# Two more products of seven in each MLP down projection of a two-layer decoder trunk, hidden parts kept for a second use, and weight pieces placed behind a norm

## The chip, the core and the metric

The kernel runs on one core of a Trainium2 chip. The engines named below are PE (TensorE, matrix products), DVE (VectorE), ACT (ScalarE), POOL (GpSimd) and SP (SyncE, which here issues the weight loads). The metric is the device time of one execution in microseconds (us), as a median over several runs.

## The reference

Two decoder layers over 256 tokens of width 2048, in float32. Layer 0 has stick-breaking attention, layer 1 differential attention over a key/value projection of its input. Each layer adds a scaled residual, normalizes, and then runs an MLP with 8192 hidden columns and normalizes again:

```python
def squared_relu_mlp(x, w_up, w_down):
    h = jax.nn.relu(x @ w_up)
    return (h * h) @ w_down
...
for layer in range(DEPTH):
    if layer < N_A_LAYERS:
        h = stick_breaking_attention(x, sb_w_qkv[layer], sb_w_o[layer])
    else:
        if layer == N_A_LAYERS:
            k_shared, v_shared = shared_kv(x, kv_w)
        ...
        h = differential_attention(x, k_shared, v_shared, ...)
    x = layer_norm(DEEPNORM_ALPHA * x + h, ln_g[layer, 0], ln_b[layer, 0])
    x = layer_norm(DEEPNORM_ALPHA * x + squared_relu_mlp(x, mlp_w_up[layer], mlp_w_down[layer]),
                   ln_g[layer, 1], ln_b[layer, 1])
```

The change touches the MLP's down projection, `(256 x 8192) @ (8192 x 2048)`, in both layers, and the seam from layer 0's last norm to layer 1's key/value projection.

## The kernel before

**Products of split numbers.** PE multiplies in a float32 form of reduced precision (fp32r). Every operand is split in two: ACT writes the high part (`split`, L60), and DVE the low part, source minus high part (L63). A product is three matmuls: high·high, high·low, low·high (`three`). For a weight the parts are called `wh` and `wl`; a load lands in `st` (four buffers, `ST_BUFS`), and `wh`, `wl` come from a ring of seven (`W_BUFS`).

**The down projection** (in `mlp`). The 8192 rows are worked in 32 pairs of 128-row groups, and the 2048 columns in two halves of 1024 (`nh` = 0, 1). `main` and `side` are accumulators in PSUM. An ordinary (classic) pair loads two pieces of 512 KB, splits them to `wh`/`wl`, splits the hidden values to `hp` (`hidden`, three buffers), and issues 24 matmuls of 128x512. For some pairs, listed in `SEVEN`, `seven` does the same 2x2 block product with seven products of three matmuls instead of eight: 21 matmuls. It needs sums and differences of the weight blocks and of the hidden values (DVE, L331 to L340), and splits of these: `hi` and `lo` of `raw` (the loaded 1 MB block, in whose last quarter the differences of hidden values are put), and `wh`, `wl` of the two halves of `sums`. `raw`, `sums`, `hi` and `lo` come from the four buffers of the tag `xT`, which hold the layer's transposed input at other times. After the last seven of a half, `share_out` adds the accumulators of `side` to the outputs with nine DVE operations. Before the change the sevens are each third pair: nine in the first half of the columns, eight in the second, 17 of 64 in a layer.

The last five pairs of the second half (`lag` = 10 groups) are worked by token block, so that the first block's output is ready early: `rest` (L377, L378) adds the residual and gathers statistics, and `layernorm` follows. Its aggregate is L139, `ve` L141, `rstd` on POOL L143, and the two halves of the normalization are L147 and L148 in four pieces of 512 columns; then PE transposes each piece (L97), and ACT and DVE split it to `xT`.

**The seam.** Layer 1 begins with the values' projection, `by_token` over `kv_w` (L639): eight chunks of weights, in four runs of two, and in each run first the products of token block t = 0 and then of t = 1. Its first matmuls run while DVE still normalizes block t = 1.

**Order.** Each engine runs its instructions in the order in which they stand in its queue. That order is set when the program is built, by the framework's scheduler from its own costs and due times; the kernel's source gives the instructions and what they depend on. Waits between engines are semaphores, buffers come from pools, and an instruction that needs a buffer waits until its last reader is done.

Of the kernel before, what the change touches and what calls it, by code (L numbers as in the profile page):

```python
# [2 lines left out]

# [8 lines left out]
ALU = mybir.AluOpType  # L12
# [17 lines left out]
RUN = 2  # L30
ST_BUFS = 4
W_BUFS = 7
SEVEN = ((3, 6, 9, 12, 15, 18, 21, 24, 27), (3, 6, 9, 12, 15, 18, 21, 24))


@with_exitstack
def trunk(ctx: ExitStack, tc: tile.TileContext, x, ln_g, ln_b, sb_w_qkv, sb_w_o, kv_w, diff_w_q,
# [96 lines left out]
    def new_stats():  # L134
        return [small.tile([P, 4, 6], F32, tag="stats", bufs=2, name=nm("stats")) for _ in range(NT)]

    def layernorm(t, stats, gb, last=False):
        mv = small.tile([P, 2], F32, tag="mv", bufs=2, name=nm("mv"))
        nc.vector.bn_aggr(mv, stats.rearrange("p a b -> p (a b)"))  # L139
        ve = small.tile([P, 1], F32, tag="ve", bufs=2, name=nm("ve"))  # L140
        nc.vector.tensor_scalar(ve, mv[:, 1:2], EPS, None, op0=ALU.add)  # L141
        rstd = small.tile([P, 1], F32, tag="rstd", bufs=2, name=nm("rstd"))
        nc.gpsimd.tensor_tensor(rstd, ve, neghalf[:, :1], op=ALU.pow)  # L143
        for j in range(4):
            sl = slice(j * 512, (j + 1) * 512)
            y = xs[:, t, sl]
            nc.vector.scalar_tensor_tensor(y, y, mv[:, 0:1], gb[j][0], op0=ALU.subtract, op1=ALU.mult)  # L147
            nc.vector.scalar_tensor_tensor(y, y, rstd, gb[j][1], op0=ALU.mult, op1=ALU.add)  # L148
# [5 lines left out]
    def mm(o, l, r, start, stop):  # L154
        nc.tensor.matmul(o, l, r, start=start, stop=stop)  # L155

    def by_token(w, n0, staggered=False, between=None):

        accs = [acc() for _ in range(NT)]
        run = RUN if staggered else 1  # L160
        for c0 in range(0, KT // 2, run):
            chunks = [
                wchunk(w[2 * c * P:(2 * c + 2) * P, n0:n0 + 512].rearrange("(a p) n -> p a n", p=P))
                for c in range(c0, c0 + run)
            ]
            for t in range(NT):
                ts = slice(t * P, (t + 1) * P)
                if between and c0 == 0 and t == 1:
                    between()
                for c, (wh, wl) in zip(range(c0, c0 + run), chunks):  # L170
                    for kk in range(2):
                        k = 2 * c + kk
                        mm(accs[t], xT[k // 4][:, k % 4, 0, ts], wh[:, kk, :], k == 0, False)
                        mm(accs[t], xT[k // 4][:, k % 4, 0, ts], wl[:, kk, :], False, False)
                        mm(accs[t], xT[k // 4][:, k % 4, 1, ts], wh[:, kk, :], False, k == KT - 1)
            tick()
        return accs
# [90 lines left out]
    def mlp(layer, last):  # L268
        up, down = mlp_w_up[layer], mlp_w_down[layer]
        with tc.tile_pool(name=f"mlp{layer}", bufs=1) as pool:  # L270
# [15 lines left out]
            def gb_of(j):  # L286
                piece = pool.tile([P, 2, 512], F32, tag="hT", bufs=FT // 4, name=nm("gb"))
                return piece[:, 0, :], piece[:, 1, :]
# [89 lines left out]
                nc.vector.bn_stats(stats[t][:, n, :], y)  # L378

            fast = SEVEN  # L380
            gb = []
            side = [acc() for _ in range(4)]
            main = [[acc("at"), acc("at")], [acc("at"), acc()]]
            for nh in range(2):
                n0 = nh * CH
                if nh == 1:
# [2 lines left out]
                        for n in range(2):  # L389
                            rest(t, n, old[t][n])  # L390
                    side = [acc("at"), acc("at"), acc("at"), acc()]
                for j in range(FT // 2 - (lag // 2 if nh else 0)):
                    k = 2 * j
                    if nh == 1 and FT // 4 < j <= FT // 4 + 4:
                        i = j - FT // 4 - 1
                        gb.append(gb_of(i))
                        for piece, src in zip(gb[i], (ln_g, ln_b)):
                            nc.vector.tensor_copy(piece[:, 0:1], hT[k // 4][:, 0, 0:1])
                            nc.sync.dma_start(piece, src[layer, 1:2, i * 512:(i + 1) * 512].broadcast_to((P, 512)))
                    if j in fast[nh]:  # L400
                        seven(k, n0, main, side, j == fast[nh][0], j == fast[nh][-1])
                        if j == fast[nh][-1]:
                            share_out(side, nh)
                        continue
                    h = hidden(k)
                    for kk in range(2):
                        wh, wl = wchunk(down[(k + kk) * P:(k + kk + 1) * P, n0:n0 + CH].rearrange(
                            "(a p) n -> p a n", p=P))
                        for t in range(NT):
                            for n in range(2):  # L410
                                ns = slice(n * 512, (n + 1) * 512)
                                three(main[t][n], [h[:, c, kk, t * P:(t + 1) * P] for c in range(2)],
                                      (wh[:, 0, ns], wl[:, 0, ns]), k + kk == 0, nh == 0 and k + kk == FT - 1)
# [109 lines left out]
    with tc.tile_pool(name="df", bufs=1) as pool:  # L523
# [112 lines left out]

        for g in range(4):
            if g == 0:
                vs = value_parts(pool, by_token(kv_w, D, True))  # L639
                background.append(lambda_to_all)  # L640
            ks, qs = keys(g), queries(g)
            vh = {}
# [51 lines left out]
```

## Time and profile before

| | |
|---|---|
| median of 3 runs | 2198.69 us (2198.13 to 2199.33) |
| profiled execution | 2199.28 us, span 2197.5 us |
| granted TensorE clock, mean | 0.998 |
| PE busy | 2176.9 us (99%) |
| DVE busy | 1579.7 us (72%) |
| ACT busy | 1112.7 us (51%) |
| `wl` of loaded weights, DVE | 700 x 1222 ns |
| `lo` of a seven, DVE | 34 x 2292 ns |
| `hp` 128x512, DVE and ACT | 94 x 686 ns and 94 x 632 ns |

The profile is one execution; its span leaves out what lies before the first and after the last instruction. A share of busy time is a mean over stages that differ: the sevens are in two stretches of the trace, about 755 to 1050 us (layer 0) and 1840 to 2140 us (layer 1), and what holds there must be read there. An engine that works far ahead of PE costs nothing; what counts is how long before PE's first read a part is written (its lead).

### The profile page before, as it was taken

To read this page: it belongs to the slowest core of one execution; us is meant where nothing else is said; L and a number is where in the kernel's file an instruction comes from. 1 tells how busy PE (TensorE), PEld (TensorE's weight loads), DVE (VectorE), ACT (ScalarE), POOL (GpSimd) and SP (SyncE) were. 2 spreads that over 40 slices of the span, in tenths; PEclk is the share of its full clock that TensorE was granted. 3 is DMA by queue.
4 is the path that set the end of the run, shared out by engine and by line. 5 is a ranking of instruction groups with operands and counts; after the bars stand their busy time and mean duration, and the time that the engine had idled before them with its cause. 6 is when DMAs were issued, how large, how long until landed. Compare 5 with 4: busy or idle time off the path is not lost.

```text
span 2197.5 us, 29466 instructions
## 1 busy us (share of the span) xinstructions
PE 2176.9 (99%) x11212; PEld 1850.2 (84%) x11212; DVE 1579.7 (72%) x2199; ACT 1112.7 (51%) x1448; POOL 14.4 (1%) x20
## 2 busy tenths in 40 slices
PE   8999999999999999999999999999999999999997
PEld 7888888888888888888888888888888888888886
DVE  5776665755555688999778786757555557899886
ACT  5665554444444455555445555535444444655652
POOL 0000000000000000000000000000000000000000
PEclk9999999999999999999999999999999999999999
DMA  7555556566666666766465555565666666666653
GB/s 267 177 157 172 165 176 226 163 190 192 190 188 190 200 201 201 234 204 208 146 210 163 173 160 186 180 213 178 189 190 191 190 189 206 198 206 210 220 188 119
DMA packets 179168, 417.83 MB, mean 190 GB/s; under 512 B 12593, under 2 KB 13105, under 8 KB 179026
## 3 DMA queue, kind: packets, MB, share of 16 engines
q1 hardware_dynamic: 175376, 409.71, 59.4%
q10 hardware_dynamic: 3650, 6.23, 0.9%
q8 instruction: 88, 1.44, 0.3%
q14 instruction: 54, 0.44, 0.1%
HBM read 413.80 MB, written 2.10 MB: 189 GB/s over the span
## 4 chain that ended last, share of the span: by engine, by line
PE 97%; DVE 1%; DMA 1%; ACT 0%; issue 0%; SPq 0%; POOL 0%; DVEq 0%; ACTq 0%
PE acc L155 82%; PE at L155 14%; PE at L97 1%; DMA st<-in_kv_w_dram 0%; DMA st<-in_sb_w_qkv_dram 0%; DVE wl L63 0%; DVE xs L148 0%; DVE xs L147 0%; PE at L624 0%; ACT wh L60 0%; PE at L597 0%; DVE xT L63 0%; PE at L278 0%; DVE stats L378 0%; DVE xs L377 0%
## 5 line engine op out<-in xcount | busy, mean ns | idle before, releaser
L63 DVE TENSOR_TENSOR wl<-st,wh 128x1024 fp32r<-128x1024 f32 x700 | 851.2, 1222 | 479.0 <-ACT wh L60 474.0
L60 ACT ACTIVATE wh<-st 128x1024 fp32r<-128x1024 f32 x700 | 736.6, 1058 | 748.8 <-PE acc L155 638.0
L155 PE MATMUL acc<-xT,wh 128*128 128x512 f32 x2944 | 1016.2, 395 | 0.4 <-ACT k L60 0.4
L155 PE MATMUL acc<-xT,wl 128*128 128x256 f32 x2944 | 789.3, 278 | 0.0
L155 PEld LDWEIGHTS acc<-xT,wh 128*128 128x128 f32 x2944 | 540.2, 188 | 113.0 <-ACT k L60 1.0
L155 PEld LDWEIGHTS acc<-xT,wl 128*128 128x128 f32 x2944 | 553.4, 188 | 16.0
L155 PE MATMUL acc<-wh,hp 128*128 128x512 f32 x984 | 320.8, 389 | 0.0
L155 PEld LDWEIGHTS acc<-wh,hp 128*128 128x128 f32 x984 | 184.6, 188 | 38.3
L155 PE MATMUL acc<-wh,xT 128*128 128x512 f32 x640 | 209.1, 395 | 1.9 <-ACT wh L60 1.8
L155 PE MATMUL at<-wh,hp 128*128 128x512 f32 x588 | 196.0, 389 | 0.0
L155 PE MATMUL acc<-wl,hp 128*128 128x512 f32 x492 | 191.5, 389 | 0.0
L60 ACT ACTIVATE hp<-hT 128x512 fp32r<-128x512 f32 (+1 forms) x128 | 76.5, 599 | 135.6 <-PE acc L155 134.1
L155 PEld LDWEIGHTS acc<-wh,xT 128*128 128x128 f32 x640 | 120.4, 189 | 27.0 <-ACT wh L60 2.1
L155 PEld LDWEIGHTS at<-wh,hp 128*128 128x128 f32 x588 | 110.4, 188 | 22.9
L155 PE MATMUL acc<-wl,xT 128*128 128x512 f32 x320 | 126.1, 394 | 0.3 <-DVE wl L63 0.3
L155 PE MATMUL at<-wl,hp 128*128 128x512 f32 x294 | 114.4, 389 | 0.0
L155 PEld LDWEIGHTS acc<-wl,hp 128*128 128x128 f32 x492 | 92.4, 188 | 19.1
L63 DVE TENSOR_TENSOR wl<-sums,wh 128x1024 fp32r<-128x1024 f32 x68 | 82.9, 1221 | 32.8 <-ACT wh L60 32.8
L60 ACT ACTIVATE wh<-sums 128x1024 fp32r<-128x1024 f32 x68 | 71.7, 1054 | 55.8 <-DVE wl L63 38.1
L63 DVE TENSOR_TENSOR lo<-raw,hi 128x2048 fp32r<-128x2048 f32 x34 | 77.9, 2292 | 16.9 <-ACT hi L60 16.8
L201 ACT ACTIVATE evb<-acc 128x256 f32<-128x256 f32 x184 | 69.0, 377 | 39.8 <-PE acc L155 34.0
L63 DVE TENSOR_TENSOR hp<-hT,hp 128x512 fp32r<-128x512 f32 (+1 forms) x128 | 82.9, 650 | 7.2 <-ACT hp L60 6.9
(162 smaller groups left out, 1869.2 us busy)
## 6 DMA issues: line engine op xcount, KB each, us to landing
st<-in_mlp_w_up_dram SPq DMA_DIRECT2D x256, 512.0 KB, 3.8
st<-in_mlp_w_down_dram SPq DMA_DIRECT2D x188, 512.0 KB, 4.7
st<-in_sb_w_qkv_dram SPq DMA_DIRECT2D x96, 512.0 KB, 4.0
raw<-in_mlp_w_down_dram SPq DMA_DIRECT2D x34, 1024.0 KB, 5.2
st<-in_kv_w_dram SPq DMA_DIRECT2D x64, 512.0 KB, 4.3
st<-in_sb_w_o_dram SPq DMA_DIRECT2D x32, 512.0 KB, 3.7
st<-in_diff_w_q_dram SPq DMA_DIRECT2D x32, 512.0 KB, 3.9
st<-in_diff_w_o_dram SPq DMA_DIRECT2D x32, 512.0 KB, 4.3
```

Of the source, the lines that this page charges most:

```text
L60: nc.scalar.activation(hi, src, AF.Copy)
L63: nc.vector.tensor_tensor(lo, src, hi.bitcast(F32), op=ALU.subtract)
L97: nc.tensor.transpose(pt[:, i * P:(i + 1) * P], src[:, i * P:(i + 1) * P], ident)
L155: nc.tensor.matmul(o, l, r, start=start, stop=stop)
L201: nc.scalar.activation(b, psum[:, T:], AF.Copy, scale=scale)
```

## The change

Three things are changed. First, `SEVEN` lists 10 positions in the first half and 9 in the second, 19 of 64 pairs in a layer; three gaps in each half have one classic pair between two sevens instead of two (9 to 11, 17 to 19, and 25 to 27 or 22 to 24). Second, the positions now count places in an order: the first half works the pairs 3 to 31 and then 2, 1, 0, the second half 2, 1, 0 first, and the `hp` parts of these three pairs are kept from one half to the next. Third, at the seam the weight pieces of the chunks 5, 6 and 7 of the values' projection get `tc.issue_after(normed[0])`: their DVE instruction (the `wl` part) is placed after the second half of the norm's piece j = 1.

```diff
-SEVEN = ((3, 6, 9, 12, 15, 18, 21, 24, 27), (3, 6, 9, 12, 15, 18, 21, 24))
+SEVEN = ((3, 6, 9, 11, 14, 17, 19, 22, 25, 27), (3, 6, 9, 11, 14, 17, 19, 22, 24))
...
+    normed = [None]
...
-            nc.vector.scalar_tensor_tensor(y, y, rstd, gb[j][1], op0=ALU.mult, op1=ALU.add)
+            done = nc.vector.scalar_tensor_tensor(y, y, rstd, gb[j][1], op0=ALU.mult, op1=ALU.add)
+            if j == 1:
+                normed[0] = done.ins
...
-    def by_token(w, n0, staggered=False, between=None):
+    def by_token(w, n0, staggered=False, between=None, behind_norm=KT):
...
+            chunks = []
+            for c in range(c0, c0 + run):
+
+                with tc.issue_after(normed[0]) if c >= behind_norm else nullcontext():
+                    chunks.append(wchunk(w[2 * c * P:(2 * c + 2) * P, n0:n0 + 512].rearrange("(a p) n -> p a n", p=P)))
...
-            gb = []
+            gb, kept = [], {}
+
+            order = (list(range(3, FT // 2)) + [2, 1, 0], [2, 1, 0] + list(range(3, (FT - lag) // 2)))
...
-                for j in range(FT // 2 - (lag // 2 if nh else 0)):
+                for i, j in enumerate(order[nh]):
...
-                    if j in fast[nh]:
-                        seven(k, n0, main, side, j == fast[nh][0], j == fast[nh][-1])
-                        if j == fast[nh][-1]:
+                    if i in fast[nh]:
+                        seven(k, n0, main, side, i == fast[nh][0], i == fast[nh][-1])
+                        if i == fast[nh][-1]:
                             share_out(side, nh)
                         continue
-                    h = hidden(k)
+                    if nh == 0 or i >= 3:
+                        kept[j] = hidden(k)
+                    h = kept[j]
...
-                vs = value_parts(pool, by_token(kv_w, D, True))
+                vs = value_parts(pool, by_token(kv_w, D, True, behind_norm=5))
```

The line numbers after the change are 3 to 5 higher: L63 and L97 stay, L147 and L148 become L149 and L150, L155 becomes L159, L331 to L340 become L336 to L345, L377 and L378 become L382 and L383.

In the rows below a line is followed by the operation, what is written, what is read, and the size; the numbers behind a name count tiles and buffers and differ between the two programs.

DVE around the last seven of the second half in layer 0 (position 24), before: `sums1688`, `raw1687` and `lo1690` are its tiles, `wl1693` and `wl1695` the low parts of its sums, and `hp1691` its hidden values; the other `wl` and `hp` belong to classic pairs.

```order
L331 TENSOR_TENSOR sums1688_9225<-raw1687_9224 128x1024
L63 TENSOR_TENSOR wl1686_9209<-st1684_9206,wh1685_9208 128x1024
L333 TENSOR_TENSOR raw1687_9224<-hT665_3721 128x256
L337 TENSOR_TENSOR sums1688_9225<-raw1687_9224,sums1688_9225 128x512
L334 TENSOR_TENSOR raw1687_9224<-raw1687_9224,hT665_3721 128x128
L63 TENSOR_TENSOR hp1680_9185<-hT664_3720,hp1680_9185 128x512
L335 TENSOR_TENSOR raw1687_9224<-hT665_3721,raw1687_9224 128x128
L340 TENSOR_TENSOR sums1688_9225<-raw1687_9224,sums1688_9225 128x512
L63 TENSOR_TENSOR wl1693_9240<-sums1688_9225,wh1692_9239 128x1024
L63 TENSOR_TENSOR wl1695_9245<-sums1688_9225,wh1694_9244 128x1024
L63 TENSOR_TENSOR lo1690_9227<-raw1687_9224,hi1689_9226 128x2048
L63 TENSOR_TENSOR hp1691_9229<-hT665_3721,hp1691_9229 128x384
```

DVE at the same seven after the change, where one classic pair stands ahead of it instead of two (`sums1689`, `raw1688`, `lo1691`; `wl1694` and `wl1696` are of its sums, `hp1692` its hidden values, `hp1699` of a classic pair):

```order
L63 TENSOR_TENSOR hp1692_9232<-hT665_3721,hp1692_9232 128x384
L336 TENSOR_TENSOR sums1689_9228<-raw1688_9227 128x1024
L338 TENSOR_TENSOR raw1688_9227<-hT665_3721 128x256
L342 TENSOR_TENSOR sums1689_9228<-raw1688_9227,sums1689_9228 128x512
L339 TENSOR_TENSOR raw1688_9227<-raw1688_9227,hT665_3721 128x128
L63 TENSOR_TENSOR wl1694_9243<-sums1689_9228,wh1693_9242 128x1024
L340 TENSOR_TENSOR raw1688_9227<-hT665_3721,raw1688_9227 128x128
L345 TENSOR_TENSOR sums1689_9228<-raw1688_9227,sums1689_9228 128x512
L63 TENSOR_TENSOR hp1699_9283<-hT665_3721,hp1699_9283 128x512
L63 TENSOR_TENSOR lo1691_9230<-raw1688_9227,hi1690_9229 128x2048
L63 TENSOR_TENSOR wl1696_9248<-sums1689_9228,wh1695_9247 128x1024
```

The seven's own `hp` stands at the start instead of at the end, only one of the two `wl` of its sums stands ahead of `lo`, and no `wl` of a classic pair stands between its operations.

DVE at the seam, before: L377 and L378 are the last of layer 0's output of block t = 1, `wl1784` and `wl1787` the low parts of the key/value weights' chunks 5 and 6:

```order
L377 TENSOR_TENSOR xs_68<-xs_68,acc1496_8213 128x512
L378 BN_STATS stats1240_6888<-xs_68 128x6
L63 TENSOR_TENSOR wl1784_9755<-st1782_9752,wh1783_9754 128x1024
L139 BN_AGGR mv1758_9607<-stats1240_6888 128x2
L63 TENSOR_TENSOR wl1787_9785<-st1785_9782,wh1786_9784 128x1024
L141 TENSOR_SCALAR ve1759_9609<-mv1758_9607 128x1
L147 SCALAR_TENSOR_TENSOR xs_68<-xs_68,mv1758_9607,gb1630_8919 128x512
L147 SCALAR_TENSOR_TENSOR xs_68<-xs_68,mv1758_9607,gb1638_8963 128x512
L148 SCALAR_TENSOR_TENSOR xs_68<-xs_68,rstd1760_9611,gb1630_8919 128x512
L148 SCALAR_TENSOR_TENSOR xs_68<-xs_68,rstd1760_9611,gb1638_8963 128x512
```

DVE at the seam, after (`wl1785`, `wl1788` and `wl1791` are of the chunks 5, 6 and 7):

```order
L382 TENSOR_TENSOR xs_68<-xs_68,acc1498_8219 128x512
L383 BN_STATS stats1240_6888<-xs_68 128x6
L141 BN_AGGR mv1759_9610<-stats1240_6888 128x2
L143 TENSOR_SCALAR ve1760_9612<-mv1759_9610 128x1
L149 SCALAR_TENSOR_TENSOR xs_68<-xs_68,mv1759_9610,gb1629_8916 128x512
L149 SCALAR_TENSOR_TENSOR xs_68<-xs_68,mv1759_9610,gb1639_8966 128x512
L150 SCALAR_TENSOR_TENSOR xs_68<-xs_68,rstd1761_9614,gb1629_8916 128x512
L150 SCALAR_TENSOR_TENSOR xs_68<-xs_68,rstd1761_9614,gb1639_8966 128x512
```

and, after a few rows of the same norm and its transposed parts, the late pieces:

```order
L149 SCALAR_TENSOR_TENSOR xs_68<-xs_68,mv1759_9610,gb1657_9060 128x512
L63 TENSOR_TENSOR wl1785_9758<-st1783_9755,wh1784_9757 128x1024
L63 TENSOR_TENSOR xT1750_9438<-at1764_9636,xT1750_9438 128x4x128
L150 SCALAR_TENSOR_TENSOR xs_68<-xs_68,rstd1761_9614,gb1657_9060 128x512
L63 TENSOR_TENSOR wl1788_9788<-st1786_9785,wh1787_9787 128x1024
L63 TENSOR_TENSOR wl1791_9794<-st1789_9791,wh1790_9793 128x1024
```

The two pieces that stood between the statistics (L378) and `ve` (L141) now stand behind the norm's first pieces, the third at its end.

PE at the seam, before: from the matmuls of chunks 4 and 5 (`acc_9672`, block t = 0) to the first transposes of block t = 1; 32 matmuls of `acc_9672` stand ahead of them:

```order
L155 MATMUL acc_9672<-wl_9749,xT_9435 128x512
L155 MATMUL acc_9672<-wh_9748,xT_9435 128x512
L155 MATMUL acc_9672<-wh_9754,xT_9435 128x512
L155 MATMUL acc_9672<-wl_9755,xT_9435 128x512
L97 MATMUL at_9615<-cst,xs 128x128 x4
L155 MATMUL acc_9672<-wh_9754,xT_9435 128x512
L97 MATMUL at_9624<-cst,xs 128x128 x4
L155 MATMUL acc_9673<-wh_9676,xT_9433 128x512
```

PE at the seam, after (`acc_9675`, block t = 0):

```order
L159 MATMUL acc_9675<-wh_9715,xT_9437 128x512
L159 MATMUL acc_9675<-wh_9721,xT_9437 128x512
L159 MATMUL acc_9675<-wl_9722,xT_9437 128x512
L159 MATMUL acc_9675<-wh_9721,xT_9437 128x512 x2
L97 MATMUL at_9618<-cst,xs 128x128 x4
L159 MATMUL acc_9675<-wl_9722,xT_9437 128x512
L97 MATMUL at_9627<-cst,xs 128x128 x4
L159 MATMUL acc_9676<-wh_9679,xT_9436 128x512
L159 MATMUL acc_9676<-wl_9680,xT_9436 128x512
```

The first transposes stand behind 22 matmuls of the values' projection instead of 32.

More of the change, by code (lines that the diff above doesn't have):

```diff
@@ L1 @@
 import math
-from contextlib import ExitStack
+from contextlib import ExitStack, nullcontext
 import concourse.bass as bass
@@ L161, in by_token @@
         for c0 in range(0, KT // 2, run):
[L162 to L165, printed above, removed]
+            chunks = []
+            for c in range(c0, c0 + run):
+                with tc.issue_after(normed[0]) if c >= behind_norm else nullcontext():
+                    chunks.append(wchunk(w[2 * c * P:(2 * c + 2) * P, n0:n0 + 512].rearrange("(a p) n -> p a n", p=P)))
             for t in range(NT):
@@ L391, in mlp @@
                     side = [acc("at"), acc("at"), acc("at"), acc()]
-                for j in range(FT // 2 - (lag // 2 if nh else 0)):
+                for i, j in enumerate(order[nh]):
                     k = 2 * j
                     if nh == 1 and FT // 4 < j <= FT // 4 + 4:
-                        i = j - FT // 4 - 1
-                        gb.append(gb_of(i))
-                        for piece, src in zip(gb[i], (ln_g, ln_b)):
+                        n = j - FT // 4 - 1
+                        gb.append(gb_of(n))
+                        for piece, src in zip(gb[n], (ln_g, ln_b)):
                             nc.vector.tensor_copy(piece[:, 0:1], hT[k // 4][:, 0, 0:1])
-                            nc.sync.dma_start(piece, src[layer, 1:2, i * 512:(i + 1) * 512].broadcast_to((P, 512)))
-                    if j in fast[nh]:
-                        seven(k, n0, main, side, j == fast[nh][0], j == fast[nh][-1])
-                        if j == fast[nh][-1]:
+                            nc.sync.dma_start(piece, src[layer, 1:2, n * 512:(n + 1) * 512].broadcast_to((P, 512)))
+                    if i in fast[nh]:
+                        seven(k, n0, main, side, i == fast[nh][0], i == fast[nh][-1])
+                        if i == fast[nh][-1]:
                             share_out(side, nh)
                         continue
-                    h = hidden(k)
+                    if nh == 0 or i >= 3:
+                        kept[j] = hidden(k)
+                    h = kept[j]
                     for kk in range(2):
@@ L412, in mlp @@
                                 three(main[t][n], [h[:, c, kk, t * P:(t + 1) * P] for c in range(2)],
-                                      (wh[:, 0, ns], wl[:, 0, ns]), k + kk == 0, nh == 0 and k + kk == FT - 1)
+                                      (wh[:, 0, ns], wl[:, 0, ns]), i + kk == 0, (nh, i, kk) == (0, FT // 2 - 1, 1))
             ks = list(range(FT - lag, FT))
```

## Prediction

> **What bounds the kernel now.** I read the page first (busy shares, clock, chain), then what PE waits for, then the chain in order of time inside the down projections, then one stretch of that stage engine by engine, and last the seam between the layers.
>
> ```profile
> span 2197.5 us, 29466 instructions
> ...
> PE 2176.9 (99%) x11212; PEld 1850.2 (84%) x11212; DVE 1579.7 (72%) x2199; ACT 1112.7 (51%) x1448; POOL 14.4 (1%) x20
> ...
> PE 97%; DVE 1%; DMA 1%; ACT 0%; issue 0%; SPq 0%; POOL 0%; DVEq 0%; ACTq 0%
> ```
>
> These are lines of the page: span; busy time of each engine; the shares of the chain that ended last. Then PE's waits (total us, times, longest):
>
> ```profile
> PE at L97 <- DMA xs<-in_x_dram: 4.8, 1, 4.8
> PE acc L155 <- ACT wh L60: 1.8, 1, 1.8
> PE at L97 <- DVE xs L148: 1.4, 1, 1.4
> PE acc L155 <- ACT k L60: 0.4, 1, 0.4
> PE acc L155 <- DVE wl L63: 0.3, 1, 0.3
> PE at L97 <- DVE xT L63: 0.3, 1, 0.3
> ```
>
> PE is 97% of the chain and waits some 9 us in all, so a change pays only by taking matmuls away or by taking one of these few waits. One of them, 1.4 us for the norm's L148, is the one that the change addresses. None lies in a down projection, where the sevens are.
>
> ```profile
> 966.92 11.56 PE acc L155 x51
> 982.56 11.56 PE acc L155 x51
> ```
>
> ```profile
> 810.36:826.00 15.64, 15.64 (x71) 12.96 (x69) 13.95 (x17) 9.41 (x10) 0.00 (x0) 1.00 0.64 202
> ```
>
> The first two are pieces of the chain (start, length): one period, a seven and two classic pairs, takes 982.56 − 966.92 = 15.64 us. The row below them is such a period in layer 0 (columns: length, busy PE, weight load, DVE, ACT, POOL, granted clock, DMA share, GB/s). A period has 21 + 2×24 = 69 matmuls, so one takes 15.64 / 69 = 0.2267 us at a clock of 1.00; a seven is 4.76 us of PE, a classic pair 5.44. PE is busy for all of it, but DVE for 13.95 us as well: it is the engine that the sevens load, and its reserve is 1.69 us a period.
>
> **The matmuls.** Four more sevens (two a layer), three matmuls fewer in each: 12 × 0.2267 = 2.72 us, all on PE, if PE never waits. To get them in, three gaps in each half of the columns (before the positions 11, 19, 27 and 11, 19, 24) hold one classic pair instead of two: 4.76 + 5.44 = 10.20 us of PE. Whether DVE and ACT keep up there is the question.
>
> ```profile
> 810.36 0.39 PE L155 MATMUL acc<-hi,hp 128*128 128x512 f32 x1
> ...
> 814.21 0.39 PE L155 MATMUL acc<-wh,lo 128*128 128x512 f32 x1
> ...
> 826.00 0.39 PE L155 MATMUL acc<-hi,hp 128*128 128x512 f32 x1
> ...
> 814.97 1.90 ACT L60 ACTIVATE hi<-raw 128x2048 fp32r<-128x2048 f32 x1
> ...
> 816.91 2.29 DVE L63 TENSOR_TENSOR lo<-raw,hi 128x2048 fp32r<-128x2048 f32 x1 [0.58 <-ACT hi L60]
> ...
> 821.86 0.69 DVE L63 TENSOR_TENSOR hp<-hT,hp 128x512 fp32r<-128x512 f32 x1
> 822.46 1.22 DVE L63 TENSOR_TENSOR wl<-st,wh 128x1024 fp32r<-128x1024 f32 x1
> 823.59 1.22 DVE L331 TENSOR_TENSOR sums<-raw 128x1024 f32<-128x1024 f32 x1
> 824.73 1.22 DVE L63 TENSOR_TENSOR wl<-st,wh 128x1024 fp32r<-128x1024 f32 x1
> 825.86 0.42 DVE L333 TENSOR_TENSOR raw<-hT 128x256 f32<-128x256 f32 x1
> 826.20 0.69 DVE L337 TENSOR_TENSOR sums<-raw,sums 128x512 f32<-128x512 f32 x1
> ```
>
> These are rows of the timeline of that period, PE's, then ACT's, then DVE's (start, length). A seven starts at 810.36, the next at 826.00. Its `lo` is done at 816.91 + 2.29 = 819.20, so in the steady state `lo` leads PE by 6.8 us. That lead is what the change spends.
>
> DVE starts one instruction after another 1.14 us (wl, sums), 0.60 (hp) and 0.34 (L333) apart, a little under their durations. A classic pair is 2 × 1.14 + 0.60 = 2.88, a seven 13.95 − 2 × 2.88 = 8.19. A short gap so asks DVE for 11.07 us in 10.20 of PE: 0.87 too much; a short and two long ones ask for 38.97 in 41.48. By work alone DVE keeps up.
>
> What binds sooner is the buffers. `raw`, `sums`, `hi` and `lo` of a seven take all four slots of one tag. `hi` of the next seven takes the slot of a `hi` or `lo` that PE reads until the 18th matmul of the seven before (814.21 is the start of that one, 3.85 after the seven's start; its 0.39 end at 4.24). In a short gap `hi` thus starts 4.3 after the previous seven at the earliest, `lo` is done at 4.3 + 1.90 + 2.29 = 8.5 or later, and the lead at a short gap is at most 10.20 − 8.5 = 1.7 us, whatever it was before. And with the new spacing the program mostly gives the next `raw` the slot of the last `raw`, which comes free when `lo` is done:
>
> ```profile
> L334 DVE TENSOR_TENSOR raw<-raw,hT x34: 281/284/288, 758.8 to 2128.6; 128x128 f32<-128x128 f32 x34
> ...
> DMA to landing us min/median/max: 4.9/5.2/9.2
> ```
>
> Of the view of `raw`'s tiles, the first row is a 128x128 step (L334; L335 is alike: 0.28, some 0.20 from start to start), the second the time from issue to landing of its transfer. The loop from one `lo` to the next is then: `raw` 5.2, sums 1.14, L333, L337 and L334 1.14, a wl 1.14 that stands between in the new order, L335 0.20, `hi` 1.90, `lo` 2.29: 13.0, with the handovers between queues some 13.3 us (an estimate). A long gap gives 15.64 − 13.3 = 2.3 us of lead back, a short one costs 10.20 − 13.3 = −3.1. Place by place: the first short gap of each half (11) is met with the lead at 6.8 and leaves some 2 (`hi` has another slot there). Ahead of 19 (both halves) and of 27 stand two long gaps; they restore 4.6, so these are met at about 6 and end at 1.7 or less. Other DVE rows that stand ahead of `lo` there take that down to an estimated 0.7 and 0.4 at the two 19s and 0.3 at 27. Ahead of 24, the last seven of the second half, only one long gap stands: 0.5 + 2.3 − 3.1 = −0.3, and the last seven's own order, with the classic pair's `hp` ahead of `lo` (0.60), makes it −0.9. I take a stall of 1.0 us there, in each layer: +2.0. Ends: 0 if the loop is a few handovers shorter, and 10.4 if no lead survives and each of the twelve short gaps stalls for the 0.87 that DVE lacks there. Below nothing is excluded, since PE does not wait in this stage today. The value lies near the lower end because five of six leads in a layer stay above nothing and DVE's work in a group fits.
>
> **Kept parts.** Six `hp` splits fewer (three a layer), about 0.6 us of ACT and of DVE each. PE waits for no `hp` now (the waits above are all there are), and ACT is busy for 9.41 of 15.64 us. The kept parts hold three `hp` buffers up to the middle of the projection; pairs 2, 1, 0 are classic there, and the second half starts on splits that are ready. Cost 0, between −0.6 and +0.6 (one split before or after a wait); the cover is the steady lead of `lo`, without which the price is one split, 0.6 us. Four loads fewer on SP with the same bytes (one 1 MB `raw` for two of 512 KB): 0. The last seven's share-out and the tail keep their positions; one L377 step now stands ahead of three late weight pieces, whose lead I count down to 0.5: 0, at worst one such step of 0.7.
>
> **The seam.** All rows are of layer 0's end.
>
> ```profile
> 1101.52 0.39 PE L155 MATMUL acc<-wh,xT 128*128 128x512 f32 x1
> ...
> 1108.55 0.39 PE L155 MATMUL acc<-wl,xT 128*128 128x512 f32 x1
> 1110.36 0.63 PE L97 MATMUL at<-cst,xs 128*128 128x128 f32 x4 [1.43 <-DVE xs L148]
> ...
> 1102.34 0.69 DVE L377 TENSOR_TENSOR xs<-xs,acc 128x512 f32<-128x512 f32 x1
> 1103.06 0.69 DVE L378 BATCH_NORM_STATS2 stats<-xs 128x6 f32<-128x512 f32 x1
> 1103.91 1.23 DVE L63 TENSOR_TENSOR wl<-st,wh 128x1024 fp32r<-128x1024 f32 x1 [0.16 <-ACT wh L60]
> 1105.06 0.26 DVE L139 BATCH_NORM_AGGREGATE mv<-stats 128x2 f32<-128x24 f32 x1
> 1106.94 1.23 DVE L63 TENSOR_TENSOR wl<-st,wh 128x1024 fp32r<-128x1024 f32 x1 [1.63 <-ACT wh L60]
> 1108.08 0.15 DVE L141 TENSOR_SCALAR ve<-mv 128x1 f32<-128x1 f32 x1
> ...
> 1109.47 1.41 DVE L148 SCALAR_TENSOR_TENSOR xs<-xs,rstd,gb 128x512 f32<-128x512 f32 x2
> ...
> 1108.37 0.92 POOL L143 TENSOR_TENSOR rstd<-ve,neghalf 128x1 f32<-128x1 f32 x1 [19.44 <-DVE ve L141]
> ```
>
> DVE handles the key/value weights' pieces in order with the second token block's norm. The piece at 1106.94 waits 1.63 us for ACT, which waits for its load, and the norm's next step, `ve` at 1108.08, is queued behind it for 2.8 us after its input was there (1105.06 + 0.26). From `ve` to the transposes, with `rstd` on POOL (0.92) and L148 between, it is 1110.36 − 1108.08 = 2.28. In the changed order both pieces stand behind the norm. Then the aggregate follows the statistics at 1103.06 + 0.72 = 1103.8, `ve` at about 1104.1, transposes possible at 1106.4. The new PE order has 22 matmuls of the first block ahead of them instead of 32: 1101.52 + 22 × 0.2267 = 1106.5. So PE does not wait: it gains the wait, 1110.36 − 1108.55 − 0.23 = 1.58 us less something at the second transposes; I take 1.5 (1.3 to 1.6), once, as only this seam has it. If the transposes come 0.1 to 0.3 late, that is in these ends. Queued behind the late pieces: chunk 5's comes some 5 us later, its matmul stands 10 and more after 1101.52, and the loads for the keys that wait for its buffer on SP land several us before their use. Cost 0; without that cover the price is a wait like the longest one today for wh, 1.8 us, which takes the gain away.
>
> **Sum.** −2.72 − 1.5 + 2.0 + 0 = −2.2 us. The profiled execution took 2199.28 (its span and 1.78 around it), 0.59 above the median of 2198.69; from the median the forecast is 2196.5, from that execution 2197.1.
>
> **Rivals.** (a) No stall: the loop through `raw` is shorter than I count, or the leads hold. For it: PE waits nowhere here now; against it: the cap of 1.7. Time: 2198.69 − 4.2 = 2194.5. (b) Several short gaps stall: the leads at 19, 19, 27 and 24 are all 1 us smaller than I have them. They then cost 0.3 + 0.6 + 0.7 + 1.9 = 3.5 in a layer, 7.0 in all: 2198.69 − 4.2 + 7.0 = 2201.5. With it go the cases in which the change does not do what it says at the seam (the transposes then wait for a load, or for a late piece, as long as today): 2198.69 − 2.7 + 2.0 = 2198.0. (c) Slower: `raw` lands late. Its slot comes free late now, so its landing time is in the loop, which it was not (the 5.2 median lay under the old lead; the longest was 9.2). Over the nine gaps from 3 to 27 PE has 9 × 4.76 + 15 × 5.44 = 124.4 us, 13.8 a gap against 13.3; with a landing of 6.6 in the mean the loop is 14.7, the lack 9 × 0.9 = 8.1 less 6 of lead, 2.1 in each of four halves: from there on the kernel is slower by over 0.2%, 2203 (2194.5 and 4 × 2.1), and 2206 at 6.7.
>
> (d) The clock. At one landing of 9.2, 4.0 over the median, the seven at 24 would stall for 1.0 + 4.0 = 5.0 us; every wait of PE in today's trace is shorter but the first (4.8), and the clock is 1.00 in the period shown. If the clock halved behind such a stall, each matmul of that seven would take 0.45 instead of 0.23 and the stall cost 5.0 + 4.8: 2196.5 + 4.0 + 4.8 = 2205.3. [...]
>
> **How the numbers follow.** My forecast (stalls of 1 to 3.5 us in all) gets 0.50, the case without stalls 0.27, several stalls 0.15, late `raw` 0.06, the clock 0.02. 0.2% of 2198.69 is 4.4 us, about what a measurement of this kernel tells from no change: below 2194.3 and above 2203.1. The case without stalls sits on the lower bound, and half of it falls under: faster 0.14. All of mine and of (b), and the rest of (a), lie within: 0.78. Slower 0.08. The range takes (a) with 0.6 below its value and some two thirds of (b), and leaves out the rest of both, (c) and (d), 0.17: 2193.9 to 2201.0.
>
> **What would show it.** Right: 12 matmuls fewer; waits of PE for `lo` or `hi` of the seven at 24, 0.5 to 1.5 us, in each layer, and next to nothing at 11, 19, 27; long gaps at 15.64, short ones at 10.2; no wait for L150 (the former L148) at the seam and the transposes some 5 us after the first key/value matmul. Wrong: a wait at 19 or 27 of over 1 us, a landing median of `raw` above 6, a clock under 1.00 in a period, a new wait on wh or wl of the key/value weights.

## The result: 17.8 us slower, and the profile after

The changed kernel takes 2216.43 us (2215.71 to 2217.96, four runs) against 2198.63 of the kernel before: a ratio of 1.0082 (95% interval 1.0064 to 1.0099). The forecast was 2196.5, in a range of 2193.9 to 2201.0. These are the lines of the page and then all waits of PE over 0.5 us (total, times, longest):

```profile
span 2216.2 us, 29396 instructions
...
PE 2182.1 (98%) x11200; PEld 1849.0 (83%) x11200; DVE 1595.5 (72%) x2221; ACT 1115.3 (50%) x1446; POOL 14.4 (1%) x20
...
PE 84%; DVE 7%; DMA 5%; ACT 2%; issue 2%; SPq 0%; DVEq 0%; POOL 0%; ACTq 0%; POOLq 0%
```

```profile
PE at L159 <- DVE lo L63: 6.0, 4, 1.8
PE at L97 <- DMA xs<-in_x_dram: 4.9, 1, 4.9
PE at L159 <- ACT hi L60: 4.9, 2, 2.7
PE acc L159 <- ACT wh L60: 2.1, 2, 1.9
PE acc L159 <- DVE lo L63: 1.8, 2, 1.5
PE acc L159 <- DVE wl L63: 1.0, 2, 0.8
PE at L283 <- ACT r L280: 0.9, 1, 0.9
PE acc L159 <- DVE hp L63: 0.6, 1, 0.6
```

PE has its 12 matmuls fewer and yet is busy for 5.2 us more (2182.1 against 2176.9): some matmuls ran slower. The chain, 97% PE before, now runs for 14% of the span through DVE, transfers and ACT; and the waits are for `hi` and `lo`, the parts of a seven. Where PE lost time is read from its matmuls' starts: whatever a start lies beyond 0.227 us after the last one is excess. Summed by place, over those beyond 0.15 us:

| place | layer 0 | layer 1 | forecast for a layer |
|---|---|---|---|
| seven at 27, first half | 0.5 | 1.6 | 0 |
| seven at 11, second half | 7.3 | 6.0 | 0 |
| seven at 19, second half | 0 | 0.3 | 0 |
| seven at 24, second half | 1.4 | 1.4 | 1.0 |
| tail of the second half | 1.9 | 1.1 | 0 |

With 0.8 us at layer 1's first transposes (L283) these are 22.3 us. Less 2.7 for the matmuls and 1.6 for the seam that makes 18.0; the median grew by 17.8, the span of the profiled execution by 18.7.

The seam did what was forecast. In this piece of PE's timeline the first key/value matmul stands at 1111.92 and the transposes of block t = 1 at 1116.91, 4.99 us later, with no wait:

```profile
1111.92 0.39 PE L159 MATMUL acc<-wh,xT 128*128 128x512 f32 x1
...
1116.91 0.60 PE L97 MATMUL at<-cst,xs 128*128 128x128 f32 x4
```

The loss is at 11 of the second half. PE's timeline there in layer 0, then the same stretch in windows (length, busy PE, weight load, DVE, ACT, POOL, granted clock, DMA share, GB/s):

```profile
987.92 0.39 PE L159 MATMUL acc<-wh,hp 128*128 128x512 f32 x1
991.00 0.60 PE L159 MATMUL at<-hi,hp 128*128 128x512 f32 x1 [2.69 <-ACT hi L60]
993.33 0.79 PE L159 MATMUL at<-lo,hp 128*128 128x512 f32 x1 [1.73 <-DVE lo L63]
993.92 0.63 PE L159 MATMUL at<-hi,hp 128*128 128x512 f32 x1
994.35 0.63 PE L159 MATMUL acc<-hi,hp 128*128 128x512 f32 x1
...
998.14 0.39 PE L159 MATMUL at<-wh,hi 128*128 128x512 f32 x1
```

```profile
978.00:987.90 9.90, 9.90 (x45) 8.21 (x44) 7.31 (x13) 2.81 (x5) 0.00 (x0) 1.00 0.49 185
987.90:993.40 5.50, 1.08 (x4) 0.26 (x2) 5.20 (x5) 5.50 (x7) 0.00 (x0) 0.81 0.38 130
993.40:997.90 4.50, 4.50 (x11) 3.53 (x12) 4.50 (x6) 1.43 (x2) 0.00 (x0) 0.50 0.83 284
997.90:1002.40 4.50, 4.50 (x21) 3.74 (x20) 4.47 (x8) 1.82 (x3) 0.00 (x0) 0.98 0.77 256
```

PE waits 2.9 us for `hi` and 2.1 for `lo`, and the matmuls behind stand 0.43 us apart (994.35 − 993.92) until 998.14: the granted clock is 0.50 there. What made `hi` late is in the chain (start, length): two loads of `raw`, 9.58 and 7.92 us long, where the median before was 5.2, and DVE waits for both.

```profile
954.58 0.37 DVE gb L405 x5
...
956.52 9.58 DMA raw<-in_mlp_w_down_dram
...
973.67 7.92 DMA raw<-in_mlp_w_down_dram
```

```profile
966.20 1.22 DVE L336 TENSOR_TENSOR sums<-raw 128x1024 f32<-128x1024 f32 x1 [2.97 <-DMA raw<-in_mlp_w_down_dram]
...
974.12 2.29 DVE L63 TENSOR_TENSOR lo<-raw,hi 128x2048 fp32r<-128x2048 f32 x1 [0.58 <-ACT hi L60]
...
981.68 1.23 DVE L336 TENSOR_TENSOR sums<-raw 128x1024 f32<-128x1024 f32 x1 [1.94 <-DMA raw<-in_mlp_w_down_dram]
...
990.98 2.29 DVE L63 TENSOR_TENSOR lo<-raw,hi 128x2048 fp32r<-128x2048 f32 x1 [0.30 <-ACT hi L60]
```

These are DVE rows on the same path. The first `raw` is issued right after the loads of the norm's gains and offsets (`gb`), whose placeholder copies (L405) stand together at 954.58; before the change they stood apart. SP's rows for the last of these loads and the `raw` behind it, before and then after:

```profile
949.28 0.38 SPq L399 DMA_DIRECT2D gb<-in_ln_b_dram  x1
953.03 0.38 SPq L319 DMA_DIRECT2D raw<-in_mlp_w_down_dram  x1
```

```profile
956.05 0.38 SPq L406 DMA_DIRECT2D gb<-in_ln_b_dram  x1
956.52 0.50 SPq L324 DMA_DIRECT2D raw<-in_mlp_w_down_dram  x1
```

One `raw` of the kernel before lands late as well, the next one (968.67, behind two `gb` loads, 7.6 us), but there the lead stays 7.1: the transfer was not in the path. After the change the `lo` of the seven at 9 is done at 976.41, and PE reads it at 978.17: a lead of 1.76 us (from the end of `lo` to the first matmul that reads it, 0.2 after the seven's first) where the forecast had 6.8.

The late loads are not all of the wait at 11. A late `hi` has a part in it, as these rows of DVE and then of ACT show:

```profile
985.70 0.28 DVE L340 TENSOR_TENSOR raw<-hT,raw 128x128 f32<-128x128 f32 x1
...
987.71 1.23 DVE L63 TENSOR_TENSOR wl<-sums,wh 128x1024 fp32r<-128x1024 f32 x1 [0.66 <-ACT wh L60]
...
986.62 1.06 ACT L60 ACTIVATE wh<-sums 128x1024 fp32r<-128x1024 f32 x1 [2.21 <-DVE sums L345]
...
989.05 1.89 ACT L60 ACTIVATE hi<-raw 128x2048 fp32r<-128x2048 f32 x1
```

The input of `hi` is complete at 985.98, but `hi` starts 3.07 us later, behind two `wh` splits and an `hp` in ACT's order and just after the last `wl` of this seven's own sums (988.94). Which of the two holds it back isn't shown. Had it started at once, the wait would have been about 2 us instead of 5 (an estimate from these rows; no run takes this delay away).

The leads of `lo` in layer 0, in us, at each seven, worked out in this way from the trace:

| | first half | second half |
|---|---|---|
| before | 10.9, then 7.0 throughout | 25.4, then 7.0 to 7.1 |
| after | 12.0, 7.0, 7.0, **2.9**, 5.8, 6.6, **0.4**, 2.9, 3.2, **0** | 6.1, 3.8, 1.8, **0**, 4.9, 5.6, **0.3**, 1.8, **0** |

Bold stands for the sevens at the end of a short gap. 0 (0.06, the handover) means that PE waited.

### The profile page after: what moved, and what is told of

It reads as the page before. It is cut to its first block, busy times and chain, and to the rows that moved or that the text cites. A ratio compares the mean times of both kernels' runs of the same rounds, so it can differ in the third digit from the quotient of the medians.

```text
span 2216.2 us, 29396 instructions
## 1 busy us (share of the span) xinstructions
PE 2182.1 (98%) x11200; PEld 1849.0 (83%) x11200; DVE 1595.5 (72%) x2221; ACT 1115.3 (50%) x1446; POOL 14.4 (1%) x20
## 4 chain that ended last, share of the span: by engine, by line
PE 84%; DVE 7%; DMA 5%; ACT 2%; issue 2%; SPq 0%; DVEq 0%; POOL 0%; ACTq 0%; POOLq 0%
PE acc L159 73%; PE at L159 10%; DVE wl L63 3%; DMA raw<-in_mlp_w_down_dram 2%; DMA st<-in_mlp_w_down_dram 2%; DVE lo L63 1%; ACT hi L60 1%; ACT wh L60 1%; PE at L97 1%; DVE hp L63 1%; DVE sums L336 1%; DVE sums L342 0%; DMA st<-in_sb_w_qkv_dram 0%; DMA st<-in_mlp_w_up_dram 0%; DVE raw L338 0%
## 5 line engine op out<-in xcount | busy, mean ns | idle before, releaser
L63 DVE TENSOR_TENSOR wl<-st,wh 128x1024 fp32r<-128x1024 f32 x692 | 839.6, 1221 | 483.0 <-ACT wh L60 478.4
L60 ACT ACTIVATE wh<-st 128x1024 fp32r<-128x1024 f32 x692 | 727.0, 1058 | 739.4 <-PE acc L159 607.3
L159 PE MATMUL acc<-xT,wh 128*128 128x512 f32 x2944 | 1016.1, 395 | 0.3 <-ACT k L60 0.3
L159 PE MATMUL acc<-xT,wl 128*128 128x256 f32 x2944 | 789.3, 278 | 0.0
L159 PEld LDWEIGHTS acc<-xT,wh 128*128 128x128 f32 x2944 | 540.3, 188 | 112.9 <-ACT k L60 1.0
L159 PEld LDWEIGHTS acc<-xT,wl 128*128 128x128 f32 x2944 | 553.4, 188 | 16.0
L159 PE MATMUL acc<-wh,hp 128*128 128x512 f32 x948 | 310.1, 390 | 0.9 <-DVE hp L63 0.6
L159 PE MATMUL acc<-wh,xT 128*128 128x512 f32 x640 | 208.5, 395 | 2.0 <-ACT wh L60 1.9
L159 PEld LDWEIGHTS acc<-wh,hp 128*128 128x128 f32 x948 | 177.7, 188 | 38.9 <-DVE hp L63 1.5
L159 PE MATMUL at<-wh,hp 128*128 128x512 f32 x568 | 189.2, 389 | 0.0
L159 PE MATMUL acc<-wl,hp 128*128 128x512 f32 x474 | 185.0, 390 | 1.0 <-DVE wl L63 1.0
L60 ACT ACTIVATE wh<-sums 128x1024 fp32r<-128x1024 f32 x76 | 80.0, 1055 | 125.9 <-DVE sums L336 90.7
L159 PEld LDWEIGHTS acc<-wh,xT 128*128 128x128 f32 x640 | 120.4, 189 | 27.0 <-ACT wh L60 2.1
L159 PE MATMUL acc<-wl,xT 128*128 128x512 f32 x320 | 126.3, 395 | 0.0
L159 PEld LDWEIGHTS at<-wh,hp 128*128 128x128 f32 x568 | 106.6, 188 | 22.1
L159 PE MATMUL at<-wl,hp 128*128 128x512 f32 x284 | 110.5, 389 | 0.0
L63 DVE TENSOR_TENSOR lo<-raw,hi 128x2048 fp32r<-128x2048 f32 x38 | 87.1, 2291 | 31.6 <-ACT hi L60 31.6
L159 PEld LDWEIGHTS acc<-wl,hp 128*128 128x128 f32 x474 | 89.0, 188 | 21.1 <-DVE wl L63 2.6
L63 DVE TENSOR_TENSOR wl<-sums,wh 128x1024 fp32r<-128x1024 f32 x76 | 92.4, 1218 | 13.1 <-ACT wh L60 13.0
L60 ACT ACTIVATE hi<-raw 128x2048 fp32r<-128x2048 f32 x38 | 72.7, 1912 | 29.8 <-DVE raw L340 13.3
```

Of the source, the lines that this page charges most:

```text
L60: nc.scalar.activation(hi, src, AF.Copy)
L63: nc.vector.tensor_tensor(lo, src, hi.bitcast(F32), op=ALU.subtract)
```

## Experiments

My theory after the result: a short gap takes most of a lead, as forecast, but the second half's first short gap is met with a lead already lost; to the new path from one `lo` through `raw` to the next, the `gb` loads add several us (9.58 and 7.92 us to landing against 5.2), and behind the wait of 5 us the granted clock is 0.50. Rivals: the kept parts; DVE's work as such; the short gap at 11 by itself. Each time below is set against runs of the kernel before on the same chip, and differences between kernels are those of their distances from it.

**One part at a time.** First the seam alone:

```diff
-                vs = value_parts(pool, by_token(kv_w, D, True))
+                vs = value_parts(pool, by_token(kv_w, D, True, behind_norm=5))
```

> Only the seam's part of the change: the weight pieces of chunks 5 to 7 behind the norm; sevens and order as before. Theory (the seam did what was forecast, the loss is in the down projections): 1.5 us faster than before, about 2197.1, no wait of PE for L150 at the seam, first transposes some 5.0 us after the first key/value matmul. Rival (the seam's gain in the changed kernel was given back later in layer 1's attention): within 0.5 of before, 2198.2 to 2199.2.

2197.79 against 2198.98 (ratio 0.9994, interval 0.9985 to 1.0003). In the trace the wait for the norm is gone; the transposes stand 1105.96 − 1100.97 = 4.99 us after the first matmul:

```profile
1100.97 0.39 PE L159 MATMUL acc<-wh,xT 128*128 128x512 f32 x1
...
1105.96 0.60 PE L97 MATMUL at<-cst,xs 128*128 128x128 f32 x4
```

The place shows a gain of 1.6 us; the time agrees with it, though its interval also holds no change. Then the kept parts alone:

```diff
+            order = (list(range(3, FT // 2)) + [2, 1, 0], [2, 1, 0] + list(range(3, (FT - lag) // 2)))
...
+                    if nh == 0 or i >= 3:
+                        kept[j] = hidden(k)
```

> Only the order with pairs 2, 1, 0 last and first and their kept parts; 17 sevens as before, no seam part. Theory (the kept parts cost nothing): within 0.7 us of before, 2198.0 to 2199.4, and the lead of lo at the second sevens of the halves stays 7.0. Rival (the kept order takes the lead away in the middle of the projection): lead of the second half's first sevens 2 to 4 us as in the changed kernel; with long gaps only, no stall and the same time, or up to 2 us slower.

2198.56 against 2198.98 (0.9999, 0.9989 to 1.0008). The leads are those of the kernel before, 25.4 at the start of the second half too. With long gaps the kept parts cost and bring nothing. And the sevens alone:

```diff
-SEVEN = ((3, 6, 9, 12, 15, 18, 21, 24, 27), (3, 6, 9, 12, 15, 18, 21, 24))
+SEVEN = ((3, 6, 9, 11, 14, 17, 19, 22, 25, 27), (3, 6, 9, 11, 14, 17, 19, 22, 24))
```

> Only the 19 sevens with their six short gaps a layer; pairs in the old order with no kept parts, no seam part. Theory (spacing alone makes the stalls: norm's parameter loads beside raw, short gap at 11 of the second half): the changed kernel's time and the seam's gain, 2217 to 2219, a stall of about 5 us at 11 of the second half in both layers with a half-speed clock behind it. Rival (the kept order is at fault): no such stall, 2200 to 2204.

2214.3 against 2198.98 (1.0071, 1.0056 to 1.0086), 2.7 to 4.7 us less than I expected. The spacing alone makes the loss, with a granted clock of 0.50 behind 11 in both layers. Its waits there are smaller (0.7 + 2.1 and 1.6 + 2.1 us) and the lead at 9 is 4.1 and 3.2 instead of 1.8 and 1.7: the kept order, free by itself, makes the place worse once the gaps are short (the seam part, the other difference, stands 100 us behind this place in layer 0). But a lead of 4.1 was not enough either: across this one gap 6.9 us of lead are lost, where the first half's gap before 11 takes 4.1. In this kernel the `raw` of 11 is issued only when the `lo` of 9 is done, and `hi` starts 2.6 us after its input.

**The loads beside `raw`.** The changed kernel without the transfers of gains and offsets in the MLPs; the tiles are filled with 1.0, so this kernel leaves out a part of the norm:

```diff
-                            nc.sync.dma_start(piece, src[layer, 1:2, n * 512:(n + 1) * 512].broadcast_to((P, 512)))
+                            nc.gpsimd.memset(piece, 1.0)
```

> The changed kernel, with the loads of the second norm's gains and offsets in both MLPs left out (POOL fills these tiles with 1.0 instead), so no such transfer runs beside the raw loads of the second half's first sevens. Theory (these transfers delay raw, whose landing is in the loop, and so take the lead before the short gap at 11): raw lands in 5 to 6 us there, the stall at 11 falls from 5 us to under 1.5 in both layers, no half-speed clock, 2203 to 2206. Rival (the short gap and DVE's order make the stall, whatever is loaded): 2214 to 2217.

2205.89 against 2198.98 (1.0033, 1.0021 to 1.0044): 6.9 us slower than before, where the whole change was 17.8 slower. In the window of 950 to 1000 us, first the landing times of `raw` in the changed kernel, then here (from the views of its tiles), and the clock behind the seven at 11 here:

```profile
DMA to landing us min/median/max: 6.1/7.8/9.6
```

```profile
DMA to landing us min/median/max: 5.1/5.5/6.0
```

```profile
983.00:990.00 7.00, 7.00 (x32) 5.81 (x31) 6.69 (x7) 5.78 (x6) 0.00 (x0) 1.00 0.66 229
```

The leads at 3, 6 and 9 are 6.9, 5.2 and 6.2 in layer 0, and at 11 they are 1.6 and, in layer 1, 1.3 instead of nothing: no wait there, near the cap of 1.7 that I had worked out, although `hi` starts 3.07 us after its input here too. The stalls at 27 (0.4 and 1.2), at 24 (1.3 and 1.5) and in the tail remain. This refutes the rival that the short gap alone makes the stall.

The same by moving the loads, with nothing left out:

```diff
-                    if nh == 1 and FT // 4 < j <= FT // 4 + 4:
-                        n = j - FT // 4 - 1
+                    if nh == 1 and j in (13, 14, 16, 21):
+                        n = (13, 14, 16, 21).index(j)
...
-                            nc.vector.tensor_copy(piece[:, 0:1], hT[k // 4][:, 0, 0:1])
+                            nc.vector.tensor_copy(piece[:, 0:1], kept[j - 1][:, 0, 0, 0:1].bitcast(F32))
```

> The changed kernel with the loads of the norm's gains and offsets in both MLPs ordered behind the seven at 11 of the second half, in four places that each have a long gap. Theory (these loads beside raw take the lead before 11): as with the loads left out, the wait at 11 is under 1.5 us, no half-speed clock, 2204 to 2208. Rival (leaving the loads out helped because less was moved, and elsewhere they cost the same): 2212 or more.

2209.37 against 2198.61 (1.0047, 1.0032 to 1.0062), between the two expectations. The stall at 11 is gone (leads 0.7 and 2.0), as the theory has it. But in layer 0, where the loads now run between 11 and 19, 19 is met with less and stalls (0.5 + 2.1 us, with a granted clock of 0.50 behind it); in layer 1, with a lead of 2.0 at 11, it does not. The stall at 27 in layer 1 is 2.1 here, ahead of any of these loads; why it is larger than in the changed kernel (1.6) isn't settled. Moving the loads freed one place, and part of the gain was lost at others.

**One half at a time.** The ten sevens of the first half with the old eight of the second:

```diff
-SEVEN = ((3, 6, 9, 11, 14, 17, 19, 22, 25, 27), (3, 6, 9, 11, 14, 17, 19, 22, 24))
+SEVEN = ((3, 6, 9, 11, 14, 17, 19, 22, 25, 27), (3, 6, 9, 12, 15, 18, 21, 24))
```

> The changed kernel with the second half's sevens at every third pair as before (eight); the ten sevens with short gaps stay in the first half: 18 in a layer. Theory: first-half leads as in the changed kernel (2.9, 0.4 to 0.6, 0.05 with a stall of 0.5 and 1.6 at 27), the second half starts with a lead of 4 to 6 and meets no short gap, so no stall at its sevens: 2198.9 - 1.4 - 1.5 + 2.1 = 2198.1. Rival (the first half's lost lead is what makes the loss later, short gap or not): stalls at the second half's third or fourth seven, 2203 or more.

2197.34 against 2198.61 (0.9993, 0.9983 to 1.0002). And the other way round:

```diff
+SEVEN = ((3, 6, 9, 12, 15, 18, 21, 24, 27), (3, 6, 9, 11, 14, 17, 19, 22, 24))
```

> The changed kernel with the first half's sevens at every third pair as before (nine); the nine sevens with short gaps stay in the second half: 18 in a layer. The loads of the norm's gains and offsets stand apart again, as before the change. Theory (the stall at 11 of the second half needs a lead already lost when it is met): the leads at 3, 6, 9 are 7 or more again, that at 11 is over 1, no half-speed clock; the stall of 1.4 at 24 and the tail's 1 to 2 us stay in each layer: 2198.9 - 1.4 - 1.5 + 5 = 2201. Rival (the short gap at 11 stalls by itself, since hi shares the slot of its own sums): 2 to 5 us in each layer there, 2206 to 2211.

2205.24 (1.0031, 1.0018 to 1.0044), above my 2201 and below the rival's 2206. So −1.3 us for the one half and +6.6 for the other make 5.3, with the seam's gain of 1.2 to 1.6 counted twice: some 7 without that. Together they cost 17.8. The 11 or so that neither has alone are most of the 13.3 of the place at 11. The leads say why. With the first half's short gaps alone the second half starts with leads of 6.1, 4.3, 2.3 in layer 0 and meets only long gaps: no stall. With the second half's alone it starts with 25.4, 7.0, 7.0, and 11 is met and left with 1.6 (1.8 in layer 1): no stall at 11, as the theory had it. What it loses is at 19 (0.7 and 0.2), at 24 (1.5 and 1.4) and in the tail.

**The clock.** The changed kernel, with 12 matmuls by a tile of zeros ahead of the seven at 11:

```diff
+                    if nh == 1 and i == 11:
+                        for _ in range(12):
+                            mm(main[1][1], nought, wh[:, 0, :512], False, False)
```

> The changed kernel with 12 matmuls by a tile of zeros (2.7 us, they add nothing to the sums) ahead of the seven at 11 of the second half in both layers, where PE waited 2.9 and 2.4 us for hi and then 2.1 for lo. Theory (the half-speed matmuls behind these waits come from PE's idleness): the first wait shrinks to under 0.5, the one for lo stays at 2.1, and the matmuls behind run at 0.23 us each, so that the seven is over 1.5 to 2.2 us earlier in each layer. Rival (they run at half speed for another reason, such as reading parts just written): the matmuls behind stay at 0.43 us.

```profile
988.78 2.02 PE L161 MATMUL acc<-wh,nought 128*128 128x512 f32 x8
990.64 0.40 PE L161 MATMUL at<-hi,hp 128*128 128x512 f32 x1
991.99 0.49 PE L161 MATMUL at<-lo,hp 128*128 128x512 f32 x1 [0.95 <-DVE lo L63]
992.32 0.39 PE L161 MATMUL at<-hi,hp 128*128 128x512 f32 x1
992.55 0.40 PE L161 MATMUL acc<-hi,hp 128*128 128x512 f32 x1
```

```profile
990.00:996.00 6.00, 5.05 (x23) 3.82 (x22) 6.00 (x6) 3.49 (x5) 0.00 (x0) 1.00 0.82 294
```

The matmuls behind the wait are 0.23 us apart and the clock is 1.00, in layer 1 too: the same parts, just as freshly written. So at 11 the half speed went with PE's idle time, in layer 0 2.69 + 1.73 us in the changed kernel and 0.95 here, and not with the fresh parts. Yet the one run took 2215.4, 16.5 over the kernel before. With PE earlier at 11, the leads behind it are 1.6 and 1.5 instead of 4.9 and 5.6, and the stalls at 19 and 24 grow by 3.2 us in layer 0. As far as one run tells, most of what the clock cost at 11 was not lost at the end: DVE's path used it to catch up.

**The same sevens without short gaps.** Every third pair throughout, no kept parts, with the seam:

```diff
+SEVEN = (tuple(range(2, 30, 3)), tuple(range(1, 26, 3)))
```

> 19 sevens a layer as in the change, but every third pair throughout: positions 2 to 29 and 1 to 25, no short gap inside a half; pairs in the old order without kept parts, with the seam part. Theory (the short gaps, met with a lead that the norm's loads and the buffers have eaten, make the loss; the sevens themselves do not): the 12 matmuls and the seam are gained, 2198.9 - 2.7 - 1.5 = 2194.7, up to 2197 if the middle (29 to 1, with share-out and eight steps of rest) or the tail stalls a little. Rival (four more sevens are more than DVE can carry, wherever they stand): 2205 or more.

2195.53 against 2198.86 (0.9985, 0.9976 to 0.9994). PE's waits are about those of the kernel before without the norm's; this list is complete:

```profile
PE at L97 <- DMA xs<-in_x_dram: 5.1, 2, 4.8
PE acc L159 <- ACT wh L60: 1.1, 1, 1.1
PE acc L159 <- ACT k L60: 0.3, 1, 0.3
PE at L97 <- DVE xT L63: 0.3, 1, 0.3
PE acc L159 <- DVE hp L63: 0.2, 1, 0.2
```

So 19 sevens are not more than DVE can carry. In the second half the leads fall to 2.1 (the `gb` loads stand together here too), which long gaps forgive. Two kernels with 18 sevens, nine and nine, then ten and eight:

```diff
+SEVEN = (tuple(range(3, 28, 3)), tuple(range(1, 26, 3)))
```

> 18 sevens a layer: positions 3 to 27 as before in the first half, 1 to 25 (nine) in the second, every third pair; old order, no kept parts, with the seam part. Theory: 6 matmuls and the seam, 2198.9 - 1.4 - 1.5 = 2196.0, with the tail, which now begins one pair after the last seven, costing 0 to 1.5. Rival (the last seven one pair nearer to the tail makes the tail's weight pieces late): 2199 or more.

```diff
+SEVEN = (tuple(range(2, 30, 3)), tuple(range(3, 25, 3)))
```

> 18 sevens a layer: positions 2 to 29 (ten) in the first half, 3 to 24 as before in the second, every third pair; old order, no kept parts, with the seam part. Theory: 6 matmuls and the seam, 2196.0, and leads of 7.0 inside the halves. Rival (the share-out after 29 and the steps of rest meet and the second half begins with lost lead): 1 to 3 us of stalls there, 2197 to 2199.

2195.44 (0.9983, 0.9974 to 0.9993) and 2196.00 (0.9987, 0.9977 to 0.9996), without a stall at a seven. All three are 2.9 to 3.4 us faster than the kernel before; among them the runs don't separate.

## Where the prediction was right and where it failed

- **The matmuls, −2.7, and the seam, −1.5.** Right: 12 fewer, and 1.6 at the seam with transposes at the forecast 4.99 us. The kernel with even gaps gains 3.3 us in time of the 4.2; those with 18 sevens and six matmuls more gain as much, so the last 1.4 us of the matmuls are not shown in time.
- **The cap at a short gap, 1.7 us.** Near where the lead was there: 1.6 and 1.3 without the `gb` loads, 1.6 and 1.8 with the second half's sevens alone, 2.0 once with the loads moved. That these are at 11, where I had another slot for `hi` and 2 us left, is in part luck: without the `gb` loads `hi` was held back there in the same way as in the changed kernel, by 3.07 us.
- **The stalls at 24, 1.0 in each layer.** Right in place; 1.4 each. At 27 I had a lead of 0.3, and the runs showed a stall of 0.5 and 1.6; at the two 19s my 0.7 and 0.4 were 0.4 and 0.3 in layer 0. The path between was not as forecast: I had each long gap give 2.3 back, but in layer 0's first half the two before 19 gave 2.9 and 0.7, the two before 27 gave 2.5 and 0.2, so 27 was met with 3.2 instead of about 6. The 0.3 at the second 19 is luck: it stands behind the stall at 11, which let the leads grow to 4.9 and 5.6; with the second half's sevens alone, without that stall, 19 itself waits (0.7 and 0.2).
- **The step that failed:** "the first short gap of each half (11) is met with the lead at 6.8". True in the first half (7.0), false in the second: 1.8 and 1.7. I took the steady lead of before for a place behind the first half's last stall, where the second half's first `lo` leads by 6 instead of 25, and where the `gb` loads run. I had weighed what the change does to the sevens' order but not which other transfers stand beside the new path; in the order these `gb` copies stand together, which I did not read. The loop failed at this place too: it lets `hi` follow the last step of `raw` at once, and at 6, 9 and 11 `hi` came 2.3, 1.7 and 3.1 us later (layer 0), behind other splits on ACT. So this gap did not take the lead from 6.8 to 2 but from 1.8 to a wait of 5.0. It cost 13.3 us against the 0 of the forecast.
- **The rivals.** Late `raw` in the path (c) and the clock (d) are the mechanisms that came, with 0.08 together; I had (c) as a mean landing of 6.6 over all gaps; the median rose only from 5.2 to 5.5. Two late loads ahead of one place with little reserve were enough. The sum for (d), a 5.0 us stall and 4.8 at half speed, was near in kind (5.0 and 2.3 in layer 0), at 11 instead of 24. That the clock halves behind such a stall was an assumption of (d): no wait inside the projections of before shows it, and the only matmuls at half speed in that trace are at its start (a granted clock of 0.50 from 13 to 15 us), behind waits of 4.81 and 1.84. The changed kernel shows 0.50 in the window at 11; the longest gap at a seven there, in one piece, is 2.9 us, and the clock was at half speed behind shorter ones too (below).
- **Kept parts and tail, 0.** Right for the kept parts alone, wrong together with short gaps, where the wait at 11 is 2.2 and 0.8 us longer with them and the seam part than without both. The tail lost 1.9 and 1.1: the last seven leaves no lead, and the nine steps of the share-out and the tail's pieces follow at once. It loses 0.4 at one place and else nothing in the kernels whose last seven keeps its lead.

Open: why the kept order makes the lead at 9 smaller with the short gaps, and how the wait at 11 divides between the late loads and the late `hi`. And the cause of the 0.8 us at layer 1's first transposes (0.6 with the `gb` loads moved) is not known.

## What to carry to other kernels

A lead is a stock: before spending it at several places, walk through them in order, with what refills it in between, and take the lead at each place from there, not from the steady state of before. When a buffer change puts a transfer into the path from one step to the next, look for every other load near it, small or rare ones too. Spend extra work evenly: the same 19 sevens at equal distances gained 3.3 us, where six short gaps a layer lost 17.8.

## What the runs showed of the hardware

Behind a wait of 2.1 us TensorE's granted clock was 0.53 at one place and 1.00 at others. It was 0.50 behind 5.0 and 4.5 us of waits in the changed kernel and behind 2.8 and 3.7 in the one with the sevens alone (each two gaps with one matmul between), but also, with the `gb` loads moved, 0.50 behind 0.5 + 2.1 us in layer 0 and 0.53 behind 2.1 us in layer 1 (1998.70 to 2002.00 us):

```profile
1996.42 0.49 PE L159 MATMUL acc<-hi,hp 128*128 128x512 f32 x1
1998.75 0.69 PE L159 MATMUL acc<-lo,hp 128*128 128x512 f32 x1 [1.83 <-DVE lo L63]
1999.23 0.63 PE L159 MATMUL acc<-hi,hp 128*128 128x512 f32 x1
```

```profile
1032.90:1036.00 3.10, 3.10 (x9) 2.38 (x8) 3.10 (x6) 3.10 (x5) 0.00 (x0) 0.50 0.60 201
```

In the kernel with the zero matmuls it stayed at 1.00 behind 0.6 + 2.1 us in both layers, and behind 2.1 alone at 11 and 24 of layer 1:

```profile
1034.00:1040.00 6.00, 4.17 (x17) 3.25 (x18) 6.00 (x5) 3.77 (x5) 0.00 (x0) 1.00 0.84 286
```

And a load of 1 MB issued right behind four of 256 KB landed in 9.58 us, where the median of such loads in the kernel before was 5.2.
